# A diffusion layer's second feed-forward product: its seven Strassen products in the order 1 3 5 7 4 2 6, and the last norm's statistics on VectorE

## The chip, the cores and the metric

The kernel runs on one core of a Trainium2 chip. The metric is the device time of one execution in microseconds (us). Before the change three runs took 1607.36, 1609.95 and 1600.29 us, median 1607.36. A further execution was run under the profiler; it took 1601.73 us.

## The reference

One layer of a hybrid backbone works on 128 context tokens and 1024 latent tokens of width 1024. A mixer (gated DeltaNet heads beside retention heads) is followed by a post-norm, then by a channel mixer and a second post-norm. The change touches only the last lines of it:

```python
x = layer_norm(ALPHA * x + g1 * y, ln1_w[l], ln1_b[l])
h = layer_norm(x) * (1.0 + sc2) + sh2
f = jnp.einsum('btf,fd->btd', jnp.square(jax.nn.relu(jnp.einsum('btd,df->btf', h, w_ff1[l]) + b_ff1[l])),
               w_ff2[l]) + b_ff2[l]
x = layer_norm(ALPHA * x + g2 * f, ln2_w[l], ln2_b[l])
```

The hidden width is 4096. `layer_norm` takes mean and variance over the 1024 features of a token.

## The kernel before

The 1152 tokens are nine row tiles of 128: tile 0 holds the context, tiles 1 to 8 the latent tokens. Every matrix product runs in three passes (`three_passes`, L1413): each operand is split into a high part, cast by ScalarE (L160), and a low part, the rest, by VectorE (L161). The passes are high by high, high by low and low by high.

Of the 32 blocks of 128 hidden features the last 26, as 13 pairs (`PAIRS`, numbers 3 to 15), go through the second product in a Strassen form: seven products of combined operands take the place of eight. The first feed-forward stage writes the seven combinations of activations of each pair to DRAM (`pair_out`, arrays HS, and HP for the context tokens). Of the last pair it does so only after the loads for the first three pairs of the second stage are issued (`ahead`, L1384).

The second stage is `second(name)` (L1437). For a product `name` it goes over the 13 pairs. `a_part` loads HS (tile `ar`, 256 KB) and splits it into `sh` and `sl`. `b_part` loads one or two blocks of `w_ff2` (tiles `br`, 256 KB each), adds or subtracts the two on VectorE (L1380), and splits the outcome into `vh` and `vl`. Products 3, 4, 1, 7 and 6 take two blocks, 5 and 2 take one. Then come 12 matmuls for four PSUM tiles `m`. Products 3, 5, 4 and 2 carry the context as well: a load `pr` of 128x128, its split `ph`, `pl`, and three matmuls into a PSUM tile `p`. When the 13 pairs are done, VectorE adds the four `m` into the accumulators `acc` of the output blocks that use the product (L1464). `INTO` lists them: products 1 to 5 go into two blocks, 6 and 7 into one, so that a joint between products has eight or four additions. The first addition into a block reads the bias row `b2`. After the last product that a block needs, `before_last` multiplies by the gate `g2` (L1426) and adds the residual `x1` (L1427).

Buffers: `m` has seven PSUM tiles and `p` one; splits of weights and activations have twelve tiles each, `ar` five, `br` six, `pr` three, `ph` six. All loads are issued by SP in one queue. A scheduler fixes the order in which each engine runs its instructions; an engine keeps to that order and waits where something isn't ready.

The first six hidden blocks come last, in plain form. `last_ff2(t)` runs 2 x 18 matmuls for row tile t, and VectorE multiplies by the gate (L1490, tile `u`) and adds into `acc` (L1491). Then the last norm: statistics, `act_normalise` on ScalarE (L255), and `finish` (L1498, L1499), which multiplies by `ln2_w` and adds `ln2_b` on VectorE. `FIN` writes down the order: F is `last_ff2`, N the normalisation, X `finish`, and the statistics are S or B. S is `act_stats` (L259): ScalarE sums the tile (L262), scales the sum (L263) and sums the squares (L264), and VectorE makes a variance of it (L265). B is `stats` (L240): VectorE's L245 twice, L247, L248 and L249. Both end with a power by GpSimd (L157). Tiles 0 to 7 have S, tile 8 has B.

Of the kernel before, what the change touches and what calls it, by code (L numbers as in the profile page):

```python
# [19 lines left out]
NCH = 9  # L20
DFF = 4096
ALPHA = 2.0 ** 0.25
FIN = "F0 S0 N0 F1 X0 S1 N1 F2 X1 S2 N2 F3 X2 S3 N3 F4 X3 S4 N4 F5 X4 S5 N5 F6 X5 S6 N6 F7 X6 S7 N7 F8 X7 B8 X8"
EB = 512
TH = 576
CH = 288
# [54 lines left out]
def layer_kernel(ctx: ExitStack, tc: tile.TileContext, A, O):  # L81
# [3 lines left out]
    def dma(out, in_):  # L85
        nc.sync.dma_start(out=out, in_=in_)  # L86
# [38 lines left out]
    def pss():  # L125
        turns["s"].append(turns["s"].pop(0))
        return pt(turns["s"][-1])
# [5 lines left out]
    X1 = dram.tile([NT, 1024], F32, name="X1")  # L133
# [19 lines left out]
    def sb(pool, shape, tag, bufs=1, dt=F32):  # L153
        return pool.tile(shape, dt, tag=tag, name=tag, bufs=bufs)
# [114 lines left out]
    def run(order, stages):  # L269

        for step in order.split():
            name, _, ahead = step.partition("^")
            if ahead:
                tc.cur_priority -= int(ahead)
            stages[name[0]](int(name[1:] or 0))
            if ahead:
                tc.cur_priority += int(ahead)
# [6 lines left out]
    with tc.tile_pool(name="start", bufs=1) as st:  # L284
# [16 lines left out]
        p = pss()  # L301
        T.transpose(p[:, 0:73], r1, ident[0:73, 0:73])
        V.tensor_copy(out=vec1, in_=p[:, 0:73])
        p = pss()
# [836 lines left out]
    HS = {p: dram.tile([7, 128, 512], F32, name=f"HS{p}") for p in range(3, NP)}  # L1141
# [104 lines left out]
    def product(name, w):  # L1246
# [12 lines left out]
    INTO = {  # L1259
        "1": (("11", 1), ("22", 1)), "2": (("21", 1), ("22", -1)), "3": (("12", 1), ("22", 1)),  # L1260
        "4": (("11", 1), ("21", 1)), "5": (("12", 1), ("11", -1)), "6": (("22", 1),), "7": (("11", 1),),
    }
# [53 lines left out]
    def pair_out(p, af, ag):  # L1316

        a11, a21, a12, a22 = (z[:, 128 + 512 * j:640 + 512 * j] for z in (af, ag) for j in range(2))
        for i, z in enumerate((af, ag)):
            dma(HP[p][i], z[:, 0:128])  # L1320
        dma(HS[p][2], a11)
        dma(HS[p][3], a22)
        s_ = next_stage()[:, 0:128]
        G.tensor_tensor(out=s_, in0=af[:, 0:128], in1=ag[:, 0:128], op=ALU.add)
        dma(HP[p][2], s_)
        for name, u, v, op_, eng in (
            (4, a11, a12, ALU.add, G), (1, a21, a22, ALU.add, V), (0, a11, a22, ALU.add, G),
            (6, a12, a22, ALU.subtract, V), (5, a21, a11, ALU.subtract, G),
        ):
            s_ = next_stage()  # L1330
            eng.tensor_tensor(out=s_, in0=u, in1=v, op=op_)
            dma(HS[p][name], s_)
# [15 lines left out]
    AHEAD = 3  # L1348
# [3 lines left out]
    def parts_of(src, tag):  # L1352
        i = turn[tag]
        turn[tag] = (i + 1) % 12
        place, n, bufs = (fe, "1", AHEAD) if i < AHEAD else (fe2, "2", 12 - AHEAD)
        hi, lo = (sb(place, [128, 512], tag + z + n, bufs, F32R) for z in "hl")
        split(hi, lo, src)
        return hi, lo

    def a_part(src):  # L1360
        raw = sb(fe, [128, 512], "ar", 5)
        dma(raw, src)
        return parts_of(raw, "s")

    def w2_raw(f, h):
        raw = sb(fe, [128, 512], "br", 6)
        dma(raw, w_ff2[128 * f:128 * f + 128, 512 * h:512 * h + 512])
        return raw
# [7 lines left out]
    def b_part(p, name):  # L1376
        u = W2[name]
        r = [w2_raw(2 * p + i, h) for i, h in u[0:2]]
        if len(r) == 2:
            V.tensor_tensor(out=r[0], in0=r[0], in1=r[1], op=u[2])  # L1380
        return parts_of(r[0], "v")

    PAIRS = range(3, NP)
    ahead = {p: (a_part(HS[p][2]), b_part(p, "3")) for p in PAIRS[0:AHEAD]}  # L1384
    pair_out(*last_pair[0])
    close_fq()
    close_w()
# [8 lines left out]
    def pm(tag="m", bufs=7):  # L1396
        return psum.tile([128, 512], F32, tag=tag, name=tag, bufs=bufs)
# [8 lines left out]
    def prompt_part(src):  # L1406
        t = sb(fp, [128, 128], "pr", 3)
        dma(t, src)
        hi, lo = sb(fp, [128, 128], "ph", 6, F32R), sb(fp, [128, 128], "pl", 6, F32R)
        split(hi, lo, t)  # L1410
        return hi, lo

    def three_passes(p, x, w, first, last):  # L1413
        for a, (i, j) in enumerate(((0, 0), (1, 0), (0, 1))):
            T.matmul(p, x[i], w[j], start=(first and a == 0), stop=(last and a == 2))  # L1415
# [5 lines left out]
    def before_last(t, h):  # L1421

        js = slice(512 * h, 512 * h + 512)
        x1 = sb(fp, [128, 512], "x1", 4)
        dma(x1, X1[128 * t:128 * t + 128, js])
        V.tensor_tensor(out=acc[t][:, js], in0=acc[t][:, js], in1=g2[min(t, 1)][:, js], op=ALU.mult)  # L1426
        V.scalar_tensor_tensor(out=acc[t][:, js], in0=x1, scalar=ALPHA, in1=acc[t][:, js], op0=ALU.mult, op1=ALU.add)  # L1427
# [3 lines left out]
    def rows():  # L1431
        nonlocal b2
        b2 = row("b2", 1, A["b_ff2"])
        for m_ in range(2):
            g2[m_] = row(f"g2{m_}", 1, GD[2 + m_:3 + m_, :])

    def second(name):  # L1437
        m = [pm() for _ in range(4)]
        for p in PAIRS:
            x, w = ahead.pop(p) if p in ahead else (a_part(HS[p][int(name) - 1]), b_part(p, name))  # L1440
            first, last = p == PAIRS[0], p == PAIRS[-1]
            for j in range(4):
                three_passes(m[j], [z[:, 128 * j:128 * j + 128] for z in x], w, first, last)
            if name in PROMPT:
                i, h, one_, end = PROMPT[name]
                if one_ and first:
                    pp[0] = pm("p", 1)
                three_passes(pp[0], prompt_part(HP[p][i]), w, one_ and first, end and last)
        if name == "3":
            rows()  # L1450
        if name in PROMPT and PROMPT[name][3]:
            h = PROMPT[name][1]
            js = slice(512 * h, 512 * h + 512)
            V.tensor_tensor(out=acc[0][:, js], in0=pp[0], in1=b2[:, js], op=ALU.add)
            before_last(0, h)
        done = []
        for j in range(4):
            for o_, sign in INTO[name]:
                t, h = (1 + j if o_[0] == "1" else 5 + j), int(o_[1]) - 1
                js = slice(512 * h, 512 * h + 512)  # L1460
                d = acc[t][:, js]
                src = b2[:, js] if (t, h) not in seen else d
                seen.add((t, h))
                V.tensor_tensor(out=d, in0=src, in1=m[j], op=ALU.add if sign > 0 else ALU.subtract)  # L1464
                if {"12": "5", "21": "2", "11": "7", "22": "6"}[o_] == name:
                    done.append((t, h))
        for z in done:
            before_last(*z)

    second("3")  # L1470
    for name in "542176":
        second(name)


# [18 lines left out]
    def finish(t, engines):  # L1493
# [20 lines left out]
    fin["trash"] = sb(fp, [128, 1024], "trash")  # L1514
    run(FIN, dict(
        F=last_ff2,
# [39 lines left out]
```

## Time and profile before

| what | us |
|---|---|
| median of three runs | 1607.36 |
| profiled execution, its own time | 1601.73 |
| its span, first to last instruction | 1599.9 |
| TensorE busy | 1500.2 |
| VectorE busy | 1046.2 |
| ScalarE busy | 745.9 |
| first matmul of the second stage starts at | 1206.7 |
| last matmul starts at | 1580.5 |

Times inside the execution count from the start of the span. A row of a timeline gives start, length, engine, line, operation, tiles, and in brackets the idle time of the engine ahead of it with what ended it. A row of waits gives the waiting instruction, what it waited for, the total, the number and the longest. A run of the same instruction is merged into one row with its count. VectorE's rows are pipelined: the length of a lone 128x512 operation is 0.69 us, and back to back they start some 0.6 us apart. The span ends 1.83 us short of the execution's own time.

### The profile page before, as it was taken

The page shows a single profiled execution, that of the slowest core. Times are in us where ns is not written, and L with a number is a line of the kernel's source. Part 1 is how long each engine was busy: PE and PEld are TensorE (multiplying, and loading weights), DVE is VectorE, ACT ScalarE, POOL GpSimd, SP SyncE. Part 2 cuts the span into 40 slices and gives each one's busy share as a digit, 9 for nine tenths or more (in the row PEclk, how much of TensorE's full clock was granted, in tenths as well). Part 3 has the DMA queues.
Part 4 walks back from the last instruction along what each step waited for, and adds up shares of the span by engine and source line. Part 5 has one row for each costly group of instructions (what it writes and reads, how often), then busy time and mean ns, then how long its engine had stood idle before and what let it go on. Part 6 is the DMA issues. An engine that isn't in the chain of part 4 may idle for free.

```text
span 1599.9 us, 26265 instructions
## 1 busy us (share of the span) xinstructions
PE 1500.2 (94%) x9597; PEld 1322.9 (83%) x9597; DVE 1046.2 (65%) x2013; ACT 745.9 (47%) x1602; POOL 336.2 (21%) x328
## 2 busy tenths in 40 slices
PE   4899999999999999999798999999998999999995
PEld 2697687898897989978678999999996887777884
DVE  4425335577875978467883576666657777698755
ACT  4612313663554554342467654555454535344343
POOL 2211021211122021101530055654551000000011
PEclk9899999999999999999899999999999999999998
DMA  9323655233123133454356944334448888888411
GB/s 347 99 67 97 182 164 169 64 85 102 43 72 96 28 77 111 120 170 139 122 161 203 279 137 155 124 128 139 154 145 268 300 281 266 278 282 283 139 53 66
DMA packets 227379, 247.81 MB, mean 155 GB/s; under 512 B 35957, under 2 KB 161890, under 8 KB 227122
## 3 DMA queue, kind: packets, MB, share of 16 engines
q1 hardware_dynamic: 227249, 246.13, 48.5%
q8 instruction: 76, 1.25, 0.3%
q14 instruction: 54, 0.43, 0.1%
HBM read 185.72 MB, written 56.15 MB: 151 GB/s over the span
## 4 chain that ended last, share of the span: by engine, by line
PE 39%; DMA 10%; DVE 9%; issue 8%; ACT 4%; POOL 2%; SPq 1%; DVEq 0%; POOLq 0%; ACTq 0%
PE d L1252 17%; PE m L1415 7%; PE mm L194 7%; DMA br<-in_w_ff_dram 3%; DMA ar<-HS 2%; DMA af<-HX 2%; PE p L1415 1%; ACT tmp L1124 1%; PE c L900 1%; DVE vl L161 1%; DMA wor<-in_w_o_dram 1%; SPq L86 1%; DVE qk L638 1%; POOL lnmv L157 1%; PE c L891 1%
## 5 line engine op out<-in xcount | busy, mean ns | idle before, releaser
L194 PE MATMUL mm<-hH,wh 128*128 128x384 f32 x696 | 248.4, 358 | 2.0 <-ACT raw L634 2.0
L194 PE MATMUL mm<-hL,wh 128*128 128x384 f32 x696 | 247.1, 355 | 0.0
L194 PE MATMUL mm<-hH,wl 128*128 128x384 f32 x696 | 246.9, 355 | 0.0
L161 DVE TENSOR_TENSOR wl<-wr,wh 128x512 fp32r<-128x512 f32 (+1 forms) x149 | 126.9, 856 | 116.2 <-ACT wh L160 107.1
L1415 PE MATMUL m<-vh,sh 128*128 128x512 f32 x460 | 180.1, 392 | 9.6 <-DVE acc L1464 6.5
L1415 PE MATMUL m<-vh,sl 128*128 128x512 f32 x460 | 179.1, 389 | 2.0 <-DVE sl L161 2.0
L1415 PE MATMUL m<-vl,sh 128*128 128x512 f32 x460 | 179.8, 391 | 0.1
L194 PEld LDWEIGHTS mm<-hH,wh 128*128 128x128 f32 x696 | 134.7, 194 | 7.4 <-ACT raw L634 2.1
L194 PEld LDWEIGHTS mm<-hL,wh 128*128 128x128 f32 x696 | 134.1, 193 | 5.6 <-issue 4.1
L194 PEld LDWEIGHTS mm<-hH,wl 128*128 128x128 f32 x696 | 134.0, 193 | 5.0 <-issue 3.7
L160 ACT CAST wh<-wr 128x512 fp32r<-128x512 f32 (+1 forms) x149 | 89.0, 613 | 78.5 <-PE mm L194 50.3
L1252 PE MATMUL d<-sh,wl 128*128 128x288 f32 x416 | 122.9, 295 | 0.5 <-DVE wl L161 0.5
L1252 PE MATMUL d<-sh,wh 128*128 128x288 f32 x416 | 122.7, 295 | 0.4 <-ACT wh L160 0.4
L1252 PE MATMUL d<-sl,wh 128*128 128x288 f32 x416 | 122.6, 295 | 0.0
L1415 PEld LDWEIGHTS m<-vh,sh 128*128 128x128 f32 x460 | 86.3, 188 | 30.0 <-DVE acc L1464 8.2
L157 POOL TENSOR_TENSOR lnmv<-lnmv,ex 128x1 f32<-128x1 f32 x36 | 25.1, 697 | 406.9 <-DVE lnmv L265 357.6
L1415 PEld LDWEIGHTS m<-vh,sl 128*128 128x128 f32 x460 | 86.4, 188 | 20.5 <-DVE sl L161 2.4
L1415 PEld LDWEIGHTS m<-vl,sh 128*128 128x128 f32 x460 | 86.3, 188 | 19.1 <-DVE vl L161 0.4
L160 ACT CAST vh<-br 128x512 fp32r<-128x512 f32 x103 | 63.5, 620 | 80.7 <-DVE br L1380 66.1
L160 ACT CAST sh<-ar 128x512 fp32r<-128x512 f32 x103 | 63.5, 619 | 61.3 <-DMA ar<-HS 32.1
L1252 PE MATMUL d<-hH,wh 128*128 128x288 f32 x312 | 91.5, 294 | 0.0
L161 DVE TENSOR_TENSOR sl<-ar,sh 128x512 fp32r<-128x512 f32 x103 | 70.3, 685 | 25.2 <-ACT sh L160 21.1
(400 smaller groups left out, 3667.8 us busy)
## 6 DMA issues: line engine op xcount, KB each, us to landing
br<-in_w_ff_dram SPq DMA_DIRECT2D x168, 256.0 KB
ar<-HS SPq DMA_DIRECT2D x91, 256.0 KB
HS<-hL SPq DMA_DIRECT2D x65, 256.0 KB
wm<-in_w_mod_dram SPq DMA_DIRECT2D x32, 512.0 KB
wr<-in_w_in_dram SPq DMA_DIRECT2D x56, 256.0 KB
af<-HX SPq DMA_DIRECT2D x20, 576.0 KB
wm<-in_w_mod_dram SPq DMA_DIRECT2D x8, 1024.0 KB
w3h<-in_w_ff_dram SPq DMA_DIRECT2D x13, 512.0 KB
```

Source lines behind the costliest of these rows:

```text
L86: nc.sync.dma_start(out=out, in_=in_)
L157: G.tensor_tensor(out=out, in0=in_, in1=ex[:, 0, 0:n], op=ALU.pow)
L160: S.copy(out=pool_hi, in_=src)
L161: V.tensor_tensor(out=pool_lo, in0=src, in1=pool_hi.bitcast(F32), op=ALU.subtract)
L194: T.matmul(p[:, 0:384], x[:, k % 4, :], y[c][:, k, :], start=(k == 0 and a == 0), stop=(k == 7 and a == 2),)
L638: V.scalar_tensor_tensor(out=y, in0=raw[:, tap:tap + 1156], scalar=vec2[:, 12 * tap + ct:12 * tap + ct + 1], in1=y, op0=ALU.mult, op1=ALU.add,
L891: T.matmul(p[:, 0:128], UP[:, m_, 0, :], r, start=True, stop=True)
L900: T.matmul(p[:, 0:128], kt[:, n, :], y2, start=True, stop=True)
L1124: S.activation(out=tmp[:, k, :], in_=p[:, 128 * k:128 * k + 128], func=AF.Identity, scale=modT[:, 32 + kk, m:m + 1], bias=modT[:, 24 + kk, ...
L1252: T.matmul(p[:, q, :], w[x][:, k, :], hs[y][:, k, CH * q:CH * q + CH], start=(k == 0 and a == 0), stop=(k == 3 and a == 2),)
L1415: T.matmul(p, x[i], w[j], start=(first and a == 0), stop=(last and a == 2))
```

## The change

The seven products are computed in the order 1 3 5 7 4 2 6 in place of 3 5 4 2 1 7 6. What hung on the first product's name (the loads ahead, the bias and gate rows) now hangs on the first of the new order, and `before_last` runs after the last product of a block in the new order. In `FIN` the statistics of tiles 0 to 7 become B.

```diff
--- before.py
+++ after.py
@@ -20,7 +20,7 @@
 NCH = 9
 DFF = 4096
 ALPHA = 2.0 ** 0.25
-FIN = "F0 S0 N0 F1 X0 S1 N1 F2 X1 S2 N2 F3 X2 S3 N3 F4 X3 S4 N4 F5 X4 S5 N5 F6 X5 S6 N6 F7 X6 S7 N7 F8 X7 B8 X8"
+FIN = "F0 B0 N0 F1 X0 B1 N1 F2 X1 B2 N2 F3 X2 B3 N3 F4 X3 B4 N4 F5 X4 B5 N5 F6 X5 B6 N6 F7 X6 B7 N7 F8 X7 B8 X8"
 EB = 512
 TH = 576
 CH = 288
@@ -1381,7 +1381,8 @@
         return parts_of(r[0], "v")
 
     PAIRS = range(3, NP)
-    ahead = {p: (a_part(HS[p][2]), b_part(p, "3")) for p in PAIRS[0:AHEAD]}
+    SECOND = "1357426"
+    ahead = {p: (a_part(HS[p][int(SECOND[0]) - 1]), b_part(p, SECOND[0])) for p in PAIRS[0:AHEAD]}
     pair_out(*last_pair[0])
     close_fq()
     close_w()
@@ -1446,7 +1447,7 @@
                 if one_ and first:
                     pp[0] = pm("p", 1)
                 three_passes(pp[0], prompt_part(HP[p][i]), w, one_ and first, end and last)
-        if name == "3":
+        if name == SECOND[0]:
             rows()
         if name in PROMPT and PROMPT[name][3]:
             h = PROMPT[name][1]
@@ -1462,13 +1463,12 @@
                 src = b2[:, js] if (t, h) not in seen else d
                 seen.add((t, h))
                 V.tensor_tensor(out=d, in0=src, in1=m[j], op=ALU.add if sign > 0 else ALU.subtract)
-                if {"12": "5", "21": "2", "11": "7", "22": "6"}[o_] == name:
+                if max((n for n in SECOND if o_ in dict(INTO[n])), key=SECOND.index) == name:
                     done.append((t, h))
         for z in done:
             before_last(*z)
 
-    second("3")
-    for name in "542176":
+    for name in SECOND:
         second(name)
 
 
```

Lines behind 1384 of the kernel before have numbers higher by one in the changed kernel until the loop at the end of `second`: L1464 is L1465, and L1490 and later are where they were.

The orders below are VectorE's. First, the joint between the first and the second product. In the kernel before it is that of products 3 and 5; `vl1_13189` and `vl1_13222` are the splits of the first two pairs of product 5, `pl` their prompt parts, and `acc` the additions of product 3:

```order
L161 TENSOR_TENSOR sl1_13183<-ar_13180,sh1_13182 128x512
L161 TENSOR_TENSOR vl1_13189<-br_13186,vh1_13188 128x512
L161 TENSOR_TENSOR pl_13207<-pr_13204,ph_13206 128x128
L161 TENSOR_TENSOR sl1_13216<-ar_13213,sh1_13215 128x512
L161 TENSOR_TENSOR vl1_13222<-br_13219,vh1_13221 128x512
L161 TENSOR_TENSOR pl_13240<-pr_13237,ph_13239 128x128
L1464 TENSOR_TENSOR acc1_12726<-b2_13162,m_12734 128x512
L1464 TENSOR_TENSOR acc5_12730<-b2_13162,m_12734 128x512
L1464 TENSOR_TENSOR acc2_12727<-b2_13162,m_12735 128x512
L1464 TENSOR_TENSOR acc6_12731<-b2_13162,m_12735 128x512
L1464 TENSOR_TENSOR acc3_12728<-b2_13162,m_12736 128x512
```

In the changed kernel the joint is that of products 1 and 3. `br_13068` is the weight of the first pair of product 3, `vl1_13074` its split:

```order
L161 TENSOR_TENSOR sl1_13065<-ar_13062,sh1_13064 128x512
L1380 TENSOR_TENSOR br_13068<-br_13068,br_13070 128x512
L161 TENSOR_TENSOR pl_13093<-pr_13090,ph_13092 128x128
L1465 TENSOR_TENSOR acc1_12726<-b2_13044,m_12734 128x512
L1465 TENSOR_TENSOR acc5_12730<-b2_13044,m_12734 128x512
L1465 TENSOR_TENSOR acc2_12727<-b2_13044,m_12735 128x512
L1465 TENSOR_TENSOR acc6_12731<-b2_13044,m_12735 128x512
L1465 TENSOR_TENSOR acc3_12728<-b2_13044,m_12736 128x512
L1465 TENSOR_TENSOR acc7_12732<-b2_13044,m_12736 128x512
L1465 TENSOR_TENSOR acc4_12729<-b2_13044,m_12737 128x512
L1465 TENSOR_TENSOR acc8_12733<-b2_13044,m_12737 128x512
L161 TENSOR_TENSOR vl1_13074<-br_13068,vh1_13073 128x512
```

Two pairs of the next product were split ahead of the additions; now none is, and the first split stands behind all eight.

Counted in the same way, the pairs of the next product whose split stands ahead of the first addition are, at the six joints in order, 2, 6, 10, 11, 10 and 11 in the kernel before (3 to 5, 5 to 4, 4 to 2, 2 to 1, 1 to 7, 7 to 6) and 0, 5, 10, 8, 11 and 11 in the changed one (1 to 3, 3 to 5, 5 to 7, 7 to 4, 4 to 2, 2 to 6).

Second, one turn of the last norm, tile 6's `finish` and tiles 7 and 8's accumulation, in the kernel before:

```order
L265 TENSOR_SCALAR lnmv_16265<-lnmv_16265 128x1
L1491 TENSOR_TENSOR acc7_12732<-u_16292,acc7_12732 128x512
L1498 TENSOR_TENSOR acc6_12731<-acc6_12731,l2w_15874 128x512 x2
L1499 TENSOR_TENSOR acc6_12731<-acc6_12731,b2_15876 128x512 x2
L1490 TENSOR_TENSOR u_16314<-m_16295,g21_13166 128x512
L1491 TENSOR_TENSOR acc7_12732<-u_16314,acc7_12732 128x512
L1490 TENSOR_TENSOR u_16349<-m_16330,g21_13166 128x512
L265 TENSOR_SCALAR lnmv_16322<-lnmv_16322 128x1
```

and in the changed one:

```order
L1498 TENSOR_TENSOR acc6_12731<-acc6_12731,l2w_15874 128x512
L1491 TENSOR_TENSOR acc7_12732<-u_16306,acc7_12732 128x512
L1499 TENSOR_TENSOR acc6_12731<-acc6_12731,b2_15876 128x512
L1498 TENSOR_TENSOR acc6_12731<-acc6_12731,l2w_15874 128x512
L245 BN_STATS lnst_16336<-acc7_12732 128x6
L1499 TENSOR_TENSOR acc6_12731<-acc6_12731,b2_15876 128x512
L1490 TENSOR_TENSOR u_16328<-m_16309,g21_13048 128x512
L1491 TENSOR_TENSOR acc7_12732<-u_16328,acc7_12732 128x512
L245 BN_STATS lnst_16336<-acc7_12732 128x6
L247 BN_AGGR lnmv_16339<-lnst_16336 128x2
L248 TENSOR_SCALAR lnmv_16339<-lnmv_16339 128x1
L249 TENSOR_SCALAR lnmv_16339<-lnmv_16339 128x1
```

L265 is gone; a tile's own L245, L247, L248 and L249 stand between its accumulation and the next tile's, and the first half's accumulation and statistics stand among the four operations of `finish`.

## The prediction

> **What bounds the kernel now.** The page comes first: it says that TensorE is the busy engine and that there is little of it to win back.
>
> ```profile
> PE 1500.2 (94%) x9597; PEld 1322.9 (83%) x9597; DVE 1046.2 (65%) x2013; ACT 745.9 (47%) x1602; POOL 336.2 (21%) x328
> ```
>
> All that the change moves lies behind 1195 us. There I read the waits of TensorE from 1190 to 1600 us, and then the same waits one by one in its timeline.
>
> ```profile
> PE m L1415 <- DVE acc L1464: 6.5, 4, 2.4
> PE m L1415 <- DVE af L1308: 3.1, 2, 2.2
> PE m L1415 <- DVE sl L161: 2.0, 1, 2.0
> PE p L1415 <- ACT ph L160: 0.9, 1, 0.9
> ...
> 1351.79 0.50 PE L1415 MATMUL m<-vh,sh 128*128 128x512 f32 x1 [0.94 <-DVE acc L1464]
> ...
> 1399.14 0.50 PE L1415 MATMUL m<-vh,sh 128*128 128x512 f32 x1 [2.37 <-DVE acc L1464]
> ...
> 1436.81 0.50 PE L1415 MATMUL m<-vh,sh 128*128 128x512 f32 x1 [2.02 <-DVE acc L1464]
> ...
> 1473.61 0.50 PE L1415 MATMUL m<-vh,sh 128*128 128x512 f32 x1 [1.14 <-DVE acc L1464]
> ```
>
> So the seven products run nearly without a hole. The four waits for `acc` stand where one product follows another (4 to 2, 2 to 1, 1 to 7, 7 to 6): a product fills four PSUM tiles, seven exist, so the fourth tile of the next product's first pair needs the first tile of the product before, which VectorE has yet to add into `acc`. The waits for `af` and `sl` (5.1 us) come from the stage before and touch nothing that the change moves.
>
> The end is another matter. The last matmul starts at 1580.5 us, the span ends at 1599.9.
>
> ```profile
> L1415 PE MATMUL m<-vl,sh x31: 388/389/389, 1560.1 to 1580.5; 128*128 128x512 f32 x31
> ...
> 1520.00:1582.00 62.00, 60.92 (x269) 50.11 (x267) 34.98 (x62) 24.56 (x39) 7.84 (x14) 1.00 0.13 51
> 1582.00:1600.00 18.00, 0.00 (x0) 0.00 (x0) 10.61 (x20) 3.83 (x6) 2.17 (x3) 0.60 0.22 88
> ```
>
> In the windows the columns are PE, PEld, DVE, ACT, POOL. The last 18 us have no matmul at all, and no engine is busy for all of it: it is a chain. VectorE's timeline shows one turn of it, tile 6's last multiply to tile 8's statistics:
>
> ```profile
> 1579.16 1.29 DVE L1498 TENSOR_TENSOR acc<-acc,l2w 128x512 f32<-128x512 f32 x2 [1.99 <-ACT acc L255]
> 1580.37 1.29 DVE L1499 TENSOR_TENSOR acc<-acc,b 128x512 f32<-128x512 f32 x2
> 1581.57 0.68 DVE L1490 TENSOR_TENSOR u<-m,g 128x512 f32<-128x512 f32 x1
> ...
> 1582.90 0.68 DVE L1490 TENSOR_TENSOR u<-m,g 128x512 f32<-128x512 f32 x1
> 1585.77 0.15 DVE L265 TENSOR_SCALAR lnmv<-lnmv 128x1 f32<-128x1 f32 x1 [2.19 <-ACT trash L264]
> 1585.85 0.68 DVE L1491 TENSOR_TENSOR acc<-u,acc 128x512 f32<-128x512 f32 x1
> 1586.56 0.69 DVE L245 BATCH_NORM_STATS2 lnst<-acc 128x6 f32<-128x512 f32 x1
> 1588.51 1.29 DVE L1498 TENSOR_TENSOR acc<-acc,l2w 128x512 f32<-128x512 f32 x2 [1.26 <-ACT acc L255]
> ...
> 1590.93 0.68 DVE L1490 TENSOR_TENSOR u<-m,g 128x512 f32<-128x512 f32 x1
> 1591.64 0.69 DVE L1491 TENSOR_TENSOR acc<-u,acc 128x512 f32<-128x512 f32 x1
> 1592.37 0.69 DVE L245 BATCH_NORM_STATS2 lnst<-acc 128x6 f32<-128x512 f32 x1
> 1593.16 0.21 DVE L247 BATCH_NORM_AGGREGATE lnmv<-lnst 128x2 f32<-128x12 f32 x1
> 1593.41 0.15 DVE L248 TENSOR_SCALAR lnmv<-lnmv 128x1 f32<-128x1 f32 x1
> 1593.48 0.14 DVE L249 TENSOR_SCALAR lnmv<-lnmv 128x1 f32<-128x1 f32 x1
> ```
>
> From one L1498 to the next is 1588.51 - 1579.16 = 9.35 us a tile. Twice in it VectorE stands still behind ScalarE: 2.19 us for the sum of squares, 1.3 to 2.0 us for the normalised tile. A tile's matmuls take less. The chain of waits shows a pair of the second product without and with a prompt part:
>
> ```profile
> 1245.59 2.75 PE m L1415 x12
> 1248.33 0.69 PE p L1415 x3
> ```
>
> That is 0.229 us a matmul, 36 x 0.229 = 8.24 us a tile. TensorE therefore runs ahead and is done early, and the tail's chain sets the end.
>
> **The change, first part: statistics of the last norm.** For tiles 0 to 7 it takes from ScalarE two passes over the tile, and from VectorE L265 with its 2.19 us wait. It adds to VectorE what tile 8 already does above: L245 twice, L247, L248, L249. By the new order a turn is: four multiplies and adds of tile t (1579.16 to 1581.57, 2.41 us), among them the first half's accumulation and statistics of the next tile (two operations at 0.605, the spacing of L1498 and L1499: 1.21), then second half, statistics and two small operations as in 1590.93 to 1593.62 (2.69), then the way through POOL and ScalarE until L1498 may start, as now from the end of L265 (1585.92) to 1588.51 (2.59; the next tile's first L1490 hides in it). Sum 8.90 us against 9.35. It stays above 8.24, so VectorE still paces the tail. The first turns have rows of their own:
>
> ```profile
> 1516.29 1.28 DVE L1491 TENSOR_TENSOR acc<-u,acc 128x512 f32<-128x512 f32 x2
> ...
> 1523.17 1.29 DVE L1498 TENSOR_TENSOR acc<-acc,l2w 128x512 f32<-128x512 f32 x2 [1.99 <-ACT acc L255]
> ...
> 1532.46 1.29 DVE L1498 TENSOR_TENSOR acc<-acc,l2w 128x512 f32<-128x512 f32 x2 [1.99 <-ACT acc L255]
> ```
>
> Tile 0 is accumulated at 1517.57; statistics 0.6 + 1.25 (1592.37 to 1593.62), then 2.59: L1498 at 1522.0. Tile 1 follows at 1522.0 + 2.41 + 0.6 + 2.69 + 2.59 = 1530.3, tile 7 six turns later at 1530.3 + 6 x 8.90 = 1583.7, and tile 8's second half at 1583.7 + 2.41 + 1.21 = 1587.3 where it now is 1590.93. All behind it is unchanged. **Term: -3.6 us.** Its bounds: -7.8 if the turn sank to TensorE's 8.24 (7 x 1.11), and +14.8 if the wait stayed and 1.85 us of statistics came on top of each of eight turns. I take the sum, since every piece of it is a row of the same operation in the same place. Behind the waiting L1498 stand only the next tile's operations, and TensorE doesn't need their PSUM tiles: it has issued its last matmul at 1580.5, when VectorE is in tile 7.
>
> The Trainium skill speaks against this part: "Perfetto Trace Analysis", section "Optimizing Scalar/DVE Operations", would hand work from VectorE to ScalarE where VectorE is saturated, not the other way. By occupancy (34.98 of 62 us against 24.56 in the window above) the change loads the busier engine, and the sum by that rule would be the +14.8 just given; the two waits in each turn say that VectorE is not saturated there, so I go by the rows.
>
> **Second part: the order of the products.** Matmuls, loads and additions are the same in number; only who waits at a joint changes. What decides is how far VectorE's fixed queue has the next product's splits ahead of the additions. Counted in pairs, that is now 2, 6, 10, 11, 10, 11 at the six joints, with waits of 0, 0, 0.94, 2.37, 2.02, 1.14. In the changed kernel it is 0 (1 to 3), 5 (3 to 5), 10 (5 to 7), 8 (7 to 4), 11 (4 to 2), 11 (2 to 6). By the nearest rows: 5 costs nothing; 10 behind a product with prompt parts 0.9, as 4 to 2 now; 8 lies between 6 and 10, 0.2; 11 with two outputs 2.4 each, as 2 to 1.
>
> The joint with 0 has no such row. There all eight additions stand ahead of the split that the new product's third matmul needs. Eight take 4.87 us:
>
> ```profile
> 1256.64 4.87 DVE L1464 TENSOR_TENSOR acc<-b,m 128x512 f32<-128x512 f32 x8 [0.76 <-PE m L1415]
> ```
>
> The first can start 9 matmuls (2.06 us) before the product's end, so they end 2.8 us behind it, the split 0.6 later; the third matmul would have been due at +0.46. That is 3.0 us, the lower end, since the order of the queue is fixed. A split and an addition for the next product stand ahead of the eight, and their loads come behind three broadcast rows (512 KB each) in SP's queue; 1.5 us for late landing makes the upper end 4.5. I take 3.7.
>
> One wait goes: the first product has no prompt part, and with it the 0.9 us for `ph`. **Term:** 3.7 + 0 + 0.9 + 0.2 + 2.4 + 2.4 = 9.6 against 6.5 + 0.9 = 7.4, **+2.2 us**, with bounds of -7.4 (no wait left) and +9.1 (2.4 at each of five joints and 4.5 at the first, less 7.4).
>
> What could break the start is supply. The first product now needs its pairs every 2.75 us in place of 3.44. The present supply there, with the waits of SP between 1215 and 1260:
>
> ```profile
> 1220.71 0.68 DVE L161 TENSOR_TENSOR vl<-br,vh 128x512 fp32r<-128x512 f32 x1
> ...
> 1226.47 0.69 DVE L161 TENSOR_TENSOR vl<-br,vh 128x512 fp32r<-128x512 f32 x1 [0.69 <-ACT vh L160]
> ...
> 1248.56 0.69 DVE L161 TENSOR_TENSOR vl<-br,vh 128x512 fp32r<-128x512 f32 x1 [0.49 <-ACT vh L160]
> ...
> SPq L86 <- DVE pl L161: 5.2, 5, 2.3
> ...
> 1220.00:1260.00 40.00, 38.04 (x162) 1.00 0.88 302
> ...
> br<-in_w_ff_dram SPq DMA_DIRECT2D x168, 256.0 KB
> ar<-HS SPq DMA_DIRECT2D x91, 256.0 KB
> ```
>
> These are the splits of pairs 4, 7 and 13: the last six took 22.1 us, 3.68 each. But 5.2 us of SP's time went into waiting for prompt buffers, which product 1 has none of. Its pair is three loads of 256 KB, 2.6 us at the window's 302 GB/s. So pair 13 would be split by 1227.2 + 6 x 2.6 = 1242.8, and TensorE, which can begin pair 4 in full at 1221.4, wants it at 1221.4 + 9 x 2.75 = 1246.2. I cost the start at nothing; the cover is these 3.4 us.
>
> The last stage's prompt parts are loaded later than now, since the six buffers for them are in use until product 2 ends. Between that and tile 0 lies product 6, 13 x 2.75 = 35.8 us, and the longest wait for such a part is 7.8:
>
> ```profile
> ACT ph L160 <- DMA pr<-HR: 13.8, 4, 7.8
> ```
>
> I cost that at nothing too; were the room gone, tile 0 and all behind it would slip by those 7.8 us.
>
> **Sum.** -3.6 + 2.2 = -1.4 us on a span of 1599.9; the profiled execution, 1601.73, becomes 1600.3. The shown median, 1607.36, lies 5.6 above the profiled execution, and four executions of the kernel average 1604.8. From that: 1604.8 - 1.4 = **1603.4 us**.
>
> **Rivals.** The joints come out clean, since the order mixes products that load 576 KB a pair with those of 768 and 832, and VectorE is in time everywhere: -7.4 and -3.6, 1593.8 us. For it: at 2 and 6 pairs ahead there is no wait now. Against it: 10 and 11 stand in the new queue as well. 15%.
>
> The first product starves: slower than before. If pairs 7 to 13 of product 1 keep coming every 3.68 us, the last is ready at 1249.2 where TensorE wants it at 1246.2: 3.0 us; product 3, which has prompt parts again, then has no lead and is fed at the same pace where it needs 3.44, 13 x 0.24 = 3.1; and the joint between them costs its upper 4.5. 1604.8 - 1.4 + 3.0 + 3.1 + 0.8 = 1610.3. It decides as soon as a pair takes more than 2.75 us. For it: the DMA share of 0.88. Against it: the waits for prompt buffers, which go. 13%.
>
> VectorE is full in the tail, and its statistics add 8 x 1.85 = 14.8: 1604.8 + 14.8 + 2.2 = 1621.8. It needs the 2.19 us wait to stay, whose releaser the change removes. 7%. It is what the Trainium skill's rule above would make of this kernel.
>
> The tail does not move, because the way through POOL and ScalarE takes up what the statistics give: 1607.0. 10%.
>
> **How the numbers follow.** The forecast has 55%. Runs of one kernel differ by 10 us (1600.29 to 1609.95), so 1% of 1607, 16 us, is about what a measurement can tell from no change. Range: from 1592 (the first rival, a little under) to 1614 (the second and a slow draw); it leaves out the saturated VectorE. Faster by over 1% means below 1591.3: with that spread a third of the first rival and a low draw of the forecast, 0.08. Slower means above 1623.4: half of the saturated case and a little of the starved one, 0.05. Between: 0.87.
>
> **What would show it.** Right: no L262 to L264; L1498 of neighbouring tiles 8.9 us apart with one wait, for L255; the last matmul near 1582.7, its distance to the end of the span down from 19.4 to about 16; a new wait of 3 to 4.5 us on `vl` at the joint of 1 and 3; two waits near 2.4 for `acc` late. Wrong: turns of 9.4 or more; waits on `br` inside product 1; any joint above 4.5 us; a difference before 1195 us.

## The result and the profile after

| | median us | lowest to highest | executions |
|---|---|---|---|
| kernel before | 1603.18 | 1594.31 to 1609.95 | 9 |
| changed kernel | 1591.86 | 1584.38 to 1597.36 | 9 |

The ratio is 0.9927, with a 95% interval of 0.9899 to 0.9955: faster by 0.7%, less than the 1% that the prediction took for the bound. The forecast was 1603.4, and the median lies just under the range's low end of 1592. The profiled execution of the changed kernel took 1597.36 us, its span 1595.5.

The two spans, 1599.9 and 1595.5, do not show the change by themselves. The second stage's first matmul starts at 1206.7 us in the kernel before and at 1216.4 in the changed one, though the computation ahead of it is the same. So I compare from there on: 393.2 us to the end of the span before, 379.1 after, **14.1 us less**. In the thirteen profiled executions of this study that first matmul starts anywhere between 1206.1 and 1216.8, and not by the order of the products: 1206.7, 1210.9 and 1213.5 in three kernels with the order before, 1206.1 to 1216.4 in six with the changed one. From there on kernels with the same code lie closer together: five with the changed order and six load buffers take 293.5 to 294.2 us up to the first matmul of the last stage, and five with the changed tail behind product 6 take 85.6 to 86.2 us from that matmul to the end. A difference of less than 1 us between two such stretches tells nothing.

TensorE's waits in the same stretch as before (what waits, for what, total, count, longest):

```profile
PE m L1416 <- DVE af L1308: 3.0, 2, 2.2
PE m L1416 <- DVE vl L161: 1.3, 1, 1.3
PE m L1416 <- ACT vh L160: 0.4, 1, 0.4
PE m L1416 <- DVE sl L161: 0.4, 1, 0.4
```

The four waits for `acc` (6.5 us) and the one for `ph` (0.9) are gone. One new pair has come, for `vl` and `vh` of the first two pairs behind the joint of products 1 and 3, 1.7 us in all.

ScalarE's waits show what holds the splits back. These are two of its waits between 1215 and 1515 us, first in the kernel before, then in the changed one:

```profile
ACT vh L160 <- DVE br L1380: 65.2, 41, 4.8
...
ACT sh L160 <- PE m L1415: 16.5, 13, 2.3
```

```profile
ACT sh L160 <- PE m L1416: 46.1, 24, 2.8
ACT vh L160 <- DVE br L1380: 32.2, 31, 2.3
```

`vh` waits for a weight that is loaded and combined, `sh` for TensorE to free one of the twelve split tiles. The first is half of what it was, the second nearly three times as long: for more of the time the splits run as far ahead as the tiles allow, and for less of it behind the loads. The room is not the same everywhere: at the joint 7 to 4 the first addition ends only 1.1 us ahead of the matmul that needs it.

The tail, one turn on VectorE, with GpSimd's and ScalarE's rows for the same tile:

```profile
1574.81 0.69 DVE L1498 TENSOR_TENSOR acc<-acc,l2w 128x512 f32<-128x512 f32 x1 [1.68 <-ACT acc L255]
1575.42 0.68 DVE L1491 TENSOR_TENSOR acc<-u,acc 128x512 f32<-128x512 f32 x1
...
1578.42 0.68 DVE L1490 TENSOR_TENSOR u<-m,g 128x512 f32<-128x512 f32 x1
...
1580.98 0.14 DVE L249 TENSOR_SCALAR lnmv<-lnmv 128x1 f32<-128x1 f32 x1
1581.04 0.68 DVE L1490 TENSOR_TENSOR u<-m,g 128x512 f32<-128x512 f32 x1
1583.40 0.69 DVE L1498 TENSOR_TENSOR acc<-acc,l2w 128x512 f32<-128x512 f32 x1 [1.68 <-ACT acc L255]
```

```profile
1581.26 0.55 POOL L157 TENSOR_TENSOR lnmv<-lnmv,ex 128x1 f32<-128x1 f32 x1 [7.76 <-DVE lnmv L249]
1581.89 0.19 POOL L254 TENSOR_TENSOR lnmv<-lnmv 128x1 f32<-128x1 f32 x1
...
1582.12 1.25 ACT L255 ACTIVATE acc<-acc,lnmv 128x1024 f32<-128x1024 f32 x1 [7.34 <-POOL lnmv L254]
```

A turn is 1583.40 - 1574.81 = 8.59 us, with the one wait for L255. From L249's end at 1581.12 to L1498 are 2.28 us. In the kernel before the same way took 2.59, and GpSimd's rows show the difference:

```profile
1586.01 0.93 POOL L157 TENSOR_TENSOR lnmv<-lnmv,ex 128x1 f32<-128x1 f32 x1 [8.16 <-DVE lnmv L265]
1587.01 0.19 POOL L254 TENSOR_TENSOR lnmv<-lnmv 128x1 f32<-128x1 f32 x1
```

The power takes 0.55 us now, 0.93 then. The last matmul starts at 1583.3, 12.2 us from the end of the span (19.4 before).

### The profile page after: what moved, and what is told of

It reads as the page before. It is cut to its first block, busy times and chain, and to the rows that moved or that the text cites. A ratio compares the mean times of both kernels' runs of the same rounds, so it can differ in the third digit from the quotient of the medians.

```text
span 1595.5 us, 26235 instructions
## 1 busy us (share of the span) xinstructions
PE 1507.1 (94%) x9597; PEld 1328.6 (83%) x9597; DVE 1057.4 (66%) x2045; ACT 724.6 (45%) x1562; POOL 333.4 (21%) x328
## 4 chain that ended last, share of the span: by engine, by line
PE 51%; DVE 10%; issue 4%; ACT 3%; DMA 2%; POOL 2%; SPq 0%; DVEq 0%; POOLq 0%; ACTq 0%
PE d L1252 18%; PE m L1416 14%; PE mm L194 7%; PE d L194 3%; PE p L1416 2%; DVE lnst L245 2%; PE c L900 1%; PE c L891 1%; PE c L884 1%; DVE qk L638 1%; PE co L915 1%; PE co L914 1%; DVE wl L161 1%; DVE acc L1491 1%; POOL lnmv L157 1%
```

## The experiments

Since the start of the stage wanders, the column that tells most is the one from its first matmul to the end of the span ("stage"), from one profiled execution each. "acc" is TensorE's wait for the joints' additions, "turn" the last full turn of the tail, from one tile's first closing multiply to the next one's.

| kernel | stage us | acc us | turn us |
|---|---|---|---|
| before | 393.2 | 6.5 | 9.35 |
| changed | 379.1 | 0 | 8.59 |
| order alone (e1_order) | 386.3 | 0 | 9.35 |
| statistics alone (e2_stats) | 386.9 | 6.6 | 8.59 |
| before, eight load buffers (e5_br8) | 385.8 | 0.3 | 9.36 |
| changed, four load buffers (e15_br4) | 403.7 | 9.7 | 8.59 |
| changed, order 1 7 6 3 5 4 2 (e6_heavy_first) | 387.1 | 0 | 8.58 |
| changed, order 1 3 5 4 2 7 6 (e9_76_last) | 383.2 | 0.4 | 8.59 |
| changed, extra operation, two SBUF inputs (e3_two_sbuf) | 382.1 | 0 | 9.09 |
| changed, extra operation, one PSUM input (e4_one_sbuf) | 377.0 | 0 | 8.16 |
| changed, no ScalarE pass (e14_no_wait) | 376.4 | 0 | 8.16 |
| order 3 1 5 7 4 2 6, eight buffers (e8_31574) | 377.6 | 0 | 8.58 |
| the two lines above together (e13_no_wait_both) | 376.0 | 0 | 8.16 |

**The two parts apart.** The first kernel is the changed one with the old `FIN`, the second the kernel before with the new `FIN`.

> The new order of the products alone; the statistics stay on ScalarE for tiles 0 to 7. Theory (the two parts are independent): from the first matmul of the second stage to the end of the last product about 293 us as in the changed kernel (300.4 before), the waits for acc at the joints gone, turns of 9.35 us in the last norm and about 92.8 us from the last product's end to the span's end; some 7 us less than before in all. Rival (the joints come out clean only because ScalarE has less to do): waits for acc of 5 us or more in total, and less than 3 us gained.

> The statistics on VectorE alone; the products in the order of before. Theory (independent parts): joints as before with about 6.5 us of waits for acc, turns near 8.6 us, about 86 us from the last product's end to the span's end instead of 92.8; some 5 to 7 us less than before. Rival (the power on GpSimd takes 0.94 us again, as in before, and its 0.55 in the changed kernel came from the order of the products): turns of 8.9 us, some 3.6 us less.

Order alone took 1597.7 us (median of 12; 0.9975 of the kernel before, 0.9945 to 1.0004), statistics alone 1594.86 (12; 0.9954, 0.9926 to 0.9982). By the stage the parts gain 6.9 and 6.3 us, 13.2 of the 14.1 that they gain together. They are independent, as expected: the one clears the joints and leaves the turn at 9.35, the other shortens the turn and leaves 6.6 us of waits for `acc`. One row of TensorE's waits from each:

```profile
PE m L1416 <- DVE vl L161: 1.2, 1, 1.2
```

```profile
PE m L1415 <- DVE acc L1464: 6.6, 3, 2.8
```

The place of the gains says the same. Up to the first matmul of the last stage it is 300.4 us before, 293.9 with the order alone, 300.6 with the statistics alone and 293.5 in the changed kernel; from there to the end it is 92.8, 92.4, 86.2 and 85.7. In whole executions the order's gain alone is not told from none, since the wandering start is larger.

**What keeps a joint free.** Eight buffers instead of six for the weight loads, in the order before:

```diff
-        raw = sb(fe, [128, 512], "br", 6)
+        raw = sb(fe, [128, 512], "br", 8)
```

> The kernel before with eight buffers for the blocks of the second weight instead of six, nothing else. Theory (at the joints the next product's splits are late because its loads find no buffer): the four waits for acc, 6.5 us, fall under 2 us, and the products take about 295 us instead of 300.4. Rival (the splits are late because of the rate of the DMA or of VectorE's own queue): 5 us or more remain.

One execution took 1598.5 us. TensorE's waits:

```profile
PE m L1415 <- DVE af L1308: 3.3, 2, 2.2
PE p L1415 <- ACT ph L160: 1.2, 1, 1.2
PE m L1415 <- DVE sl L161: 0.4, 1, 0.4
```

With the order of products unchanged, and with 2, 6, 10, 11, 11 and 11 pairs ahead of the additions (2, 6, 10, 11, 10 and 11 in the kernel before), the waits for `acc` are gone but for 0.3 us (one matmul, at 1435.34, starts 0.53 us after the one ahead of it and not 0.23). The number of pairs ahead therefore does not set the wait. What the eight buffers change is how early a load finds a free buffer: between 1215 and 1510 us SyncE waits 8.3 us for a split `vl` to free one, where it waited 22.4, and ScalarE's wait for a loaded and combined weight falls from 65.2 to 40.4. The reverse, four buffers in the changed kernel (`"br", 4`):

> The changed kernel with four buffers for the weight loads in place of six; pairs split ahead at the joints are 0, 6, 10, 7, 11 and 11 where the changed kernel has 0, 5, 10, 8, 11 and 11. Theory (a joint costs something when the last split ahead is late against the freeing of its buffer, and fewer load buffers make it late): waits for acc come back at the joints with 10 and 11 pairs, 2 us or more in all. Rival (order and counts alone keep the joints free): no wait for acc above 0.5 us, as in the changed kernel.

One execution took 1611.61 us; the waits for `acc` are back:

```profile
PE m L1416 <- ACT vh L160: 9.8, 4, 5.1
PE m L1416 <- DVE acc L1465: 9.7, 4, 5.0
```

The joint 5 to 7 has ten pairs ahead in both kernels, and shows how the wait comes about. First VectorE and TensorE in the changed kernel, then with four buffers:

```profile
1347.03 0.68 DVE L161 TENSOR_TENSOR vl<-br,vh 128x512 fp32r<-128x512 f32 x1
1347.63 1.88 DVE L1465 TENSOR_TENSOR acc<-acc,m 128x512 f32<-128x512 f32 x3
...
1351.71 0.39 PE L1416 MATMUL m<-vh,sh 128*128 128x512 f32 x1
```

```profile
1353.94 0.69 DVE L161 TENSOR_TENSOR vl<-br,vh 128x512 fp32r<-128x512 f32 x1 [0.76 <-ACT vh L160]
1355.21 0.69 DVE L1380 TENSOR_TENSOR br<-br 128x512 f32<-128x512 f32 x1 [0.58 <-DMA br<-in_w_ff_dram]
1355.82 0.68 DVE L161 TENSOR_TENSOR sl<-ar,sh 128x512 fp32r<-128x512 f32 x1
1356.42 1.88 DVE L1465 TENSOR_TENSOR acc<-acc,m 128x512 f32<-128x512 f32 x3
...
1352.37 0.39 PE L1416 MATMUL m<-vl,sh 128*128 128x512 f32 x1
1357.75 0.80 PE L1416 MATMUL m<-vh,sh 128*128 128x512 f32 x1 [5.00 <-DVE acc L1465]
```

The matmuls at 1351.71 and 1357.75 are the first into product 7's fourth tile, which needs the first addition. In the changed kernel that addition is done at 1348.3, 3.4 us in time. With four buffers TensorE is due at 1352.6, and VectorE still stands in the operations ahead of the addition, behind a load; the addition starts 3.8 us after that. ScalarE's waits with four buffers, from 1345 to 1358 us and then, ahead of the joint 4 to 2, from 1426 to 1440, tell the two cases apart:

```profile
ACT vh L160 <- DVE br L1380: 8.4, 4, 2.9
```

```profile
ACT sh L160 <- PE m L1416: 7.2, 4, 2.1
```

At the joint 4 to 2, with eleven pairs ahead, even four buffers give no wait: product 2 loads one block a pair, and by then the splits wait for TensorE to free tiles and not for loads. The joints 3 to 5 and 7 to 4 do wait there, 1.5 and 1.2 us, with only six and seven pairs ahead.

**Which feature of the order matters.** Two kernels with other orders, `SECOND = "1763542"` and `"1354276"`.

> The changed kernel with the products in the order 1 7 6 3 5 4 2: the three that load 768 KB a pair and have no prompt part follow each other at the start. Theory (a run of heavy products is what makes splits late): TensorE waits 8 us or more in the second stage beyond the 5 us that come from the stage before, in product 1 to 6 or at their joints. Rival (what counts is that the first product has no prompt part and the heavy ones don't stand at the end): under 3 us of waits, as in the changed kernel.

> The changed kernel with the order 1 3 5 4 2 7 6: products 7 and 6, which have no prompt part and take two weight blocks, stand together at the end, behind the joint 2 to 7 with eight additions and ten gate and residual steps. Pairs ahead at the joints: 0, 5, 9, 11, 11, 10. Theory (TensorE goes through a product without prompt part in 2.75 us a pair, so that VectorE cannot make up in product 7 for the time lost at the joint before it, and the last splits ahead come late): a wait for acc of 1 to 3 us at 7 to 6, and 0 to 1 at the others. Rival (it is the start with product 1 that clears the joints, by whatever means): no wait for acc above 0.5 us. Second rival (the count of pairs ahead): waits of 1 to 2.4 at each of the joints with 9 to 11 pairs, 4 to 8 us in all.

They took 1601.65 and 1601.67 us, in one execution each. Neither of my theories held. With the three two-block products without a prompt part ahead there is no joint with a wait for `acc` L1465 at all; that stage loses 2.6 us to `vl` at the first joint, some 2.4 to matmuls that start 0.43 us apart behind that wait (see the last section) and 0.8 to the prompt tile. Its end comes 88.0 us after the first matmul of the last stage and not 85.7, which I put down to product 2, with eight blocks to finish, being the last; no run tests that. With 7 and 6 at the end the joint 7 to 6 cost 0.2, not 1 to 3:

```profile
PE m L1416 <- DVE sl L161: 2.0, 1, 2.0
PE m L1416 <- DVE vl L161: 2.0, 1, 2.0
PE p L1416 <- DVE acc L1455: 0.9, 1, 0.9
PE m L1416 <- DVE acc L1465: 0.4, 2, 0.2
```

All three orders that begin with product 1 have nearly clean joints; the order that begins with 3 and ends in 2 1 7 6 has 6.5 and, in the kernel with the statistics alone, 6.6 us. The rival noted for 1 3 5 4 2 7 6, that the start with product 1 clears the joints, gave the right number. But the orders differ in more than their start, and whether it is that or the place of 1 beside 7 and 6 is not settled; nor is it shown by what way the new order lets six buffers keep up.

**Why the power is shorter.** In the changed kernel VectorE runs L1490 beside the power, or nothing, and L1490 has one input in PSUM; in the kernel before it ran L1491 there, with both in SBUF. Both experiments add one VectorE operation behind L249 in the statistics of all nine tiles, whose result nobody uses; the second reads a PSUM tile in place of one half of `x`.

```diff
+        if "trash" in fin:
+            V.scalar_tensor_tensor(
+                out=fin["trash"][:, 0:512], in0=x[:, 0:512], scalar=mv[:, 1:2], in1=x[:, 512:1024], op0=ALU.mult, op1=ALU.add,
+            )
```

> The changed kernel with one more VectorE operation of 128x512 behind the last small operation of each tile's statistics, both of whose inputs lie in SBUF and whose result nobody uses. Theory (GpSimd's power at L157 is slowed by a VectorE operation with two SBUF inputs that runs beside it): the eight powers take 0.9 us or more where the changed kernel has 0.55, and turns of the tail go from 8.59 to about 8.95, the spacing that the prediction had. Rival (the power's 0.55 comes from what went before it, statistics by VectorE instead of ScalarE): the powers stay at 0.55 and turns at 8.6, since VectorE stands idle there for 1.7 us and the extra operation takes 0.7.

> As the kernel with the extra operation of two SBUF inputs, but one of the two inputs lies in PSUM. Theory of the two SBUF inputs: powers stay near 0.55 us and turns at 8.6 to 8.7. Rival (any further VectorE work beside the power slows it): 0.9 here as well, turns near 8.95.

One execution each, 1597.13 and 1586.96 us. With two SBUF inputs, VectorE's operation and the power in two turns:

```profile
1535.20 0.78 DVE L252 SCALAR_TENSOR_TENSOR trash<-acc,lnmv 128x512 f32<-128x512 f32 x1
...
1579.45 0.75 DVE L252 SCALAR_TENSOR_TENSOR trash<-acc,lnmv 128x512 f32<-128x512 f32 x1
```

```profile
1535.25 0.55 POOL L157 TENSOR_TENSOR lnmv<-lnmv,ex 128x1 f32<-128x1 f32 x1 [7.03 <-DVE lnmv L249]
...
1579.56 1.05 POOL L157 TENSOR_TENSOR lnmv<-lnmv,ex 128x1 f32<-128x1 f32 x1 [7.77 <-DVE lnmv L249]
```

And with one input in PSUM:

```profile
1562.05 0.75 DVE L252 SCALAR_TENSOR_TENSOR trash<-p,lnmv,acc 128x512 f32<-128x512 f32 x1
...
1562.16 0.55 POOL L157 TENSOR_TENSOR lnmv<-lnmv,ex 128x1 f32<-128x1 f32 x1 [7.34 <-DVE lnmv L249]
```

At 1579.56 the power ends at 1580.61, 0.41 us behind the end of L252 at 1580.20. In the kernel before it ends at 1586.94, 0.41 behind the end of L1491 at 1586.53. With an input in PSUM it takes 0.55 as if alone. The first theory holds, with one addition that I had not foreseen: in three of the nine turns (at 1535.25, say) the power starts only 0.05 us behind VectorE's operation, not 0.11, and keeps its 0.55. The Trainium skill, "SBUF — State Buffer", section "SBUF: two separate sides", has a rule for this: VectorE with two SBUF inputs and GpSimd share a pair of ports as an exclusive lock, and whoever starts first holds it for the whole instruction, while the other is blocked. The trace agrees where VectorE started 0.10 us or more ahead: the power then ends 0.41 us behind VectorE's operation each time. In the three other turns VectorE's operation takes 0.77 to 0.78 us in place of 0.75, so a block of VectorE for the whole of the power does not show. The turn grew by the same 0.50 that the power did, 8.59 to 9.09; I had expected 8.95.

The kernel with the order 1 7 6 3 5 4 2 has both cases in its tail with nothing added. In four of its eight turns L1491 had started ahead of the power, which took 0.87 to 0.93 us, and the way from L249 to L1498 was 2.59 or 2.60; in the other four the power took 0.55 and the way was 2.21 to 2.28.

The control kernel gave a surprise: its turn is 8.16, shorter than the changed kernel's. The extra operation moved tile t+1's first L1490 and L1491 (there L1494 and L1495) into the wait, ahead of the multiplies, and the turn is then TensorE's pace, 36 matmuls of 0.227 us.

**Taking the way through GpSimd off the turn.** If the way through GpSimd and ScalarE sets the turn, then finishing every tile as tile 8 is finished should take it off: `FIN` without the N steps, and `finish` without its branch for tiles below 8, so that the first two operations need only the mean.

```diff
-        if t < 8:
-            for j, js in halves:
-                engines[j].tensor_tensor(out=u[:, js], in0=u[:, js], in1=fin["l2w"][:, js], op=ALU.mult)
-                engines[j].tensor_tensor(out=u[:, js], in0=u[:, js], in1=fin["l2b"][:, js], op=ALU.add)
-            dma(yrow(t), u)
-            return
```

> The changed kernel without the normalisation pass on ScalarE: each tile is finished in the form that tile 8 has, so that the first two operations behind the statistics need only the mean, and VectorE has work while GpSimd computes the power. Theory (the turn of 8.59 us is the way from the statistics through GpSimd and ScalarE, 1.7 us of it with VectorE idle, and TensorE's 36 matmuls are the next bound): no wait for ScalarE is left in the tail, the tail runs at TensorE's pace of 8.16 to 8.24 us a tile, powers of 0.9 us or more beside the two-input operations cost nothing, and from the start of the stage to the end of the span it is 374 to 377 us against 379.1 in the changed kernel. Rival (VectorE, with 12 operations of 0.6 to 0.7 us a tile, is what paces the tail): turns stay at 8.5 or more and the stage at 379 or more.

```profile
1568.17 1.41 DVE L1497 SCALAR_TENSOR_TENSOR acc<-acc,lnmv,l2w 128x512 f32<-128x512 f32 x2
...
1573.71 0.69 DVE L1490 TENSOR_TENSOR u<-m,g 128x512 f32<-128x512 f32 x1 [0.88 <-PE m L1416]
...
1576.32 1.42 DVE L1497 SCALAR_TENSOR_TENSOR acc<-acc,lnmv,l2w 128x512 f32<-128x512 f32 x2
```

The turn is 1576.32 - 1568.17 = 8.15 us, VectorE's only wait is for TensorE's `m`, and the powers take 0.99 to 1.06 us without costing anything. The stage went from 379.1 to 376.4; the one execution, 1591.97, is not told from the changed kernel's time. The other way to gain, one pair ahead at the first joint and more buffers, and both together:

> The changed kernel with the order 3 1 5 7 4 2 6 and eight buffers for the weight loads in place of six; a candidate for beating both. Theory (a joint costs something when the last split that stands ahead of the additions is ready late against the freeing of its buffer; with this order one pair is split ahead at the first joint and none is left out): no wait of TensorE for acc above 0.5 us at any joint, none for vl above 1 us, first matmul of the stage to the end of the span 377 to 379 us against 379.1 in the changed kernel, time 0 to 2 us below it. Rival (product 3 with its prompt parts first is fed more slowly, as in the kernel before): waits for ph and sl in the first product of 2 to 3 us, and no gain over the changed kernel.

> The same with the order 3 1 5 7 4 2 6 and eight buffers for the weight loads. Theory (the two gains lie in different places and add up): stage to end 373 to 375.5 us, time 0.988 to 0.991 of the kernel before. Rival (the end is then set by something common to both, such as the last output's way to DRAM): no more than 1 us below the kernel with eight buffers alone, ratio 0.992 or above.

The first has no wait for `acc` or `vl`, a stage of 377.6 and 1588.66 us (median of 4; 0.9916 of the kernel before, 0.9884 to 0.9948). Together they give 376.0 and 1587.83 (6; 0.9907, 0.9875 to 0.9939), the lowest median of this study, but its interval overlaps that of the changed kernel, and 376.0 is just outside the 373 to 375.5 that I had expected: of the 1.5 and 2.7 us that the two gain apart, 3.1 of 4.2 are left together, a shortfall hardly above the spread.

## Why the prediction was wrong, point by point

**The base was right.** The prediction took 1604.8 for the kernel before, and nine executions now have a median of 1603.18. The error is in the change: -1.4 us forecast, -11.3 in the medians, -14.1 by the stage.

**The joint term failed: +2.2 forecast, -5.8 measured in the waits that it counts** (order alone: 7.4 us before, 1.6 with the new order; -6.9 by the whole stage). The step at fault is "What decides is how far VectorE's fixed queue has the next product's splits ahead of the additions. Counted in pairs". The mechanism behind it is right (the first addition stands behind those splits, and TensorE's fourth tile behind the addition), but I priced it by the count, and took 0.9 and 2.4 us from the kernel before as if they belonged to 10 and 11 pairs. The runs give 0.3 us in all for the old order with eight buffers, and 5.0 against 0 for one joint with ten pairs. What decides is when the last split ahead is ready, and the runs with more and fewer load buffers moved that by the supply of weights. The joints with 10, 8, 11 and 11 pairs cost nothing, where I had 5.9.

**The first joint was cheaper: 3.7 forecast, 1.7 measured** (1.6 to 2.6 in the six kernels with this joint and six load buffers). VectorE did what I said. Its rows there:

```profile
1256.14 4.87 DVE L1465 TENSOR_TENSOR acc<-b,m 128x512 f32<-128x512 f32 x8
1260.92 0.68 DVE L161 TENSOR_TENSOR vl<-br,vh 128x512 fp32r<-128x512 f32 x1
```

The split ends at 1261.60, 3.7 us behind the start of product 3's first matmul at 1257.91. But I let "the third matmul" of product 3 need it, and TensorE's fixed order had been rearranged as well: it puts ten matmuls that need only the weight's high part `vh` ahead of the first on `vl`. I had looked at VectorE's order at that joint and not at TensorE's.

```profile
1259.96 0.40 PE L1416 MATMUL p<-vh,pl 128*128 128x512 f32 x1
1261.66 1.20 PE L1416 MATMUL m<-vl,sh 128*128 128x512 f32 x4 [1.30 <-DVE vl L161]
```

**The tail term had the right mechanism and too small a size: -3.6 forecast, -6.3 by the stage and -6.6 from the first matmul of the last stage** (statistics alone). The turn was to be 8.90 and is 8.59. All the pieces came out but one: the way from the statistics to L1498, "as now ... (2.59)", is 2.28, since the new neighbour of GpSimd's power has an input in PSUM. Over the eight tiles that is 2.5 of the missing 2.7 to 3.0 us.

**What cost nothing was costed right.** Product 1 did not starve: the only wait inside it in TensorE's list, behind those for `af`, is 0.4 us for `sl` in its fourth pair, where the first product of the kernel before waited 2.0. No later wait for a prompt part shows either.

**The rivals.** The first, joints that come out clean, is nearly what happened; its 1593.8 us lies 2 us from the median, and it had 15%. Its -7.4 for the joints was a little too much and its -3.6 for the tail too little. Its argument was half of the truth: the other half, that a wait at ten pairs is a wait for supply, was there to be read in ScalarE's wait for `br`, 66.1 us between 1190 and 1600 us, the first row of the view from which the prediction took its line for `pr`. I had that view and did not use the row. The starving first product, the full VectorE and the unmoved tail did not come. The rule that I weighed from the Trainium skill ("Perfetto Trace Analysis", "Optimizing Scalar/DVE Operations", hand work off a saturated VectorE) does not apply here: with the statistics on VectorE its wait for L255 is still 1.68 us a turn.

**The signs.** L262 to L264 are gone, L1498 has one wait per turn, and no difference lies ahead of the stage but the wandering start. The last matmul starts at 1583.3 where 1582.7 was named, an agreement by accident, since the stage began 9.7 us later. The distance to the end is 12.2, not 16; the two waits of 2.4 for `acc` are missing. The range fell short below because it held the clean joints only with the tail that I had worked out, and nothing for a shorter one on top.

## What to carry to other kernels

A wait behind a fixed queue is priced by when the last entry ahead of it is ready, not by how many entries there are; look first whether the producer waits for free buffers (then it is on time) or for loads (then buffers or order buy time). When a scheduler rearranges one engine at a joint, read the order of the engine that waits as well. And where a chain passes through GpSimd, ask which VectorE operation stands beside it: an operation with two SBUF inputs that started 0.1 to 0.2 us earlier made GpSimd's power, and the way through it, 0.3 to 0.5 us longer here.

## What the runs showed of the hardware

- GpSimd's power on 128x1 values takes 0.55 us beside a VectorE operation with a PSUM input and 0.87 to 1.06 beside one with two SBUF inputs that started 0.10 to 0.23 us ahead of it; it then ends 0.41 us behind it.
- After a wait TensorE sometimes runs slowly for a few microseconds. With four buffers, behind the wait of 5.0 us, neighbouring matmuls start 0.43 us apart in place of 0.23, and the granted clock from 1357 to 1363 us is 0.50:

```profile
1358.77 0.63 PE L1416 MATMUL m<-vl,sh 128*128 128x512 f32 x1
1359.20 0.63 PE L1416 MATMUL m<-vh,sh 128*128 128x512 f32 x1
1359.63 0.63 PE L1416 MATMUL m<-vh,sl 128*128 128x512 f32 x1
```

  In the changed kernel this happens ahead of the fourth pair of product 1, whose wait for `sl` is then 0.4 us where the kernel before, at a granted clock of 1.00 from 1211 to 1220 us, waited 2.0; it cost nothing there. The waits of 2.0 to 2.4 us at the joints of the kernel before were not followed by it, one of 2.8 at a joint with the statistics alone was. What decides is not shown.
- The time at which identical code reaches the second stage differed by 10.7 us between thirteen executions. What makes it so was not looked into.
